# The first norm's shift and scale as TensorE products with blocks of mod_w as the stationary operand

## The chip, the cores and the metric

One NeuronCore of a Trainium2 chip runs the whole kernel. The metric is the device time of one execution in microseconds (us), the median of several runs. The engines are TensorE (PE; its weight loads stand apart as PEld), VectorE (DVE), ScalarE (ACT), GpSimd (POOL) and SyncE (SP), whose queue issues most transfers.

## What is computed

One layer of a hybrid encoder on x of 1024 tokens by 1024 columns, f32. Only its first lines matter here:

```python
mod = (jax.nn.silu(c) @ mod_w[l] + mod_b[l])[:, None, :]
sh1, sc1, g1, sh2, sc2, g2 = jnp.split(mod, 6, axis=-1)
h = rms_norm(x, norm_mix_w[l]) * (1.0 + sc1) + sh1
proj = h @ w_in[l]
...
```

c is one vector of 1024, mod_w is 1024 x 6144. What follows (gated DeltaNet heads, sparse attention, output projection, 32 experts) takes some 2600 us and needs h first. sh1 and sc1 are the first 2048 columns of mod.

## The kernel before

The host lays mod_w out as 24 blocks of [128, 8, 256]: block n holds columns 256n to 256n+255, partition p and index k together are row 128k + p. A block is 1 MB and comes in one transfer. Blocks 0 to 7 make the shift (0 to 3) and the scale (4 to 7) of the first norm, in `phase1`; blocks 8 to 23 are used later, by `later_mod`, while the projections run.

The silu of c lies in a [128, 8] tile (cs2, also self.cs), column k for rows 128k to 128k+127. The matrix-vector product of a block is made in two steps. `gemv` (line 563) multiplies each of the 8 slices [128, 256] by its column of cs2 and adds them into two accumulators (gacc): the first slice of each on ACT (line 574), the other six on DVE (line 572). Then PE sums over the partitions: for each half j of the block and each accumulator h, a product with 128 columns of the accumulator as the stationary operand and a column of ones as the moving one (line 277), so that 128 results stand down the partitions of a PSUM tile of 16 columns, `pab` (named "big" in the profile, as the pool's other tiles). That is 4 products for a block, 32 in all.

Behind the 8 blocks DVE adds the bias to `pab` (ab, line 287) and makes the scale (sca, line 289). The input x comes in 8 tiles of 128 tokens (x0 to x7). `norm` handles four of them: a square with a sum on ACT (junk, line 256), the reciprocal root in 13 short operations on DVE (`rstd`, result rs), the scaling of x on ACT (line 259). PE transposes the scaled tiles (line 317); ACT applies scale and shift to each transposed row of 512 tokens (hrow, line 319); DVE splits it into a high and a low part (hTh, hTl). With these the small projection (w_small, lines 198 to 200, as three products each) and then the index queries follow, half by half of the tokens.

The blocks use three buffers: blocks 2 and 5 one of their own (raw3), the others the pool's two (raw), which the weights w_small and w_in use next. A transfer into a buffer waits until the last reader of it is done, and SP issues its transfers in order.

Each engine works through its own list in order. The lists are not the order of the code: a scheduler of the programming layer places each instruction by its own estimate of when its operands are there.

Of the kernel before, what the change touches and what calls it, by code (L numbers as in the profile page):

```python
# [10 lines left out]
F32 = mybir.dt.float32  # L11
# [3 lines left out]
AF = mybir.ActivationFunctionType  # L15
# [5 lines left out]
P = 128  # L21
# [3 lines left out]
KD = D // P  # L25
# [109 lines left out]
class K:  # L135
# [66 lines left out]
    def phase1(self):  # L202
        nc, tc, A = self.nc, self.tc, self.A
        with ExitStack() as es:
            hp = es.enter_context(self.pool("p1h", 1))
            raw = es.enter_context(self.pool("p1raw", 2))
# [4 lines left out]
            st = esA.enter_context(self.pool("p1a", 2))  # L211
# [40 lines left out]
            def norm(half):  # L252
                s = slice(4 * half, 4 * half + 4)
                for i in range(4 * half, 4 * half + 4):
                    junk = st.tile([P, D], F32, name="junk", bufs=1)
                    nc.scalar.activation(junk, xs[i], AF.Square, accum_out=ss[:, i:i + 1])
                self.rstd(rs[:, s], ss[:, s], 1.0 / D, st)
                for i in range(4 * half, 4 * half + 4):
                    nc.scalar.activation(xs[i], xs[i], AF.Copy, scale=rs[:, i:i + 1])
# [9 lines left out]
            pab = pbig.tile([P, T], F32, name="big")  # L269

            for n in range(8):
                for i in ([0], [1], [2], [3], [], [], [], [])[n]:
                    nc.sync.dma_start(xs[i], A['x'][i * P:(i + 1) * P, :])
                acc = self.gemv(raw, st, n, 2)
                for j in range(2):
                    for h in range(2):
                        nc.tensor.matmul(pab[:, 2 * n + j:2 * n + j + 1], acc[:, h, j * P:(j + 1) * P], self.ones,
                                         start=(h == 0), stop=(h == 1))
                if n == 3:
                    norm(0)  # L280
            w_small = load_w(A['w_small'], 96)
# [29 lines left out]
            for half in range(2):  # L311

                c = slice(512 * half, 512 * half + 512)
                for k in range(KD):
# [3 lines left out]
                    h = st.tile([P, 512], F32, name="hrow", bufs=3)  # L318
# [12 lines left out]
            st = esB.enter_context(self.pool("p1b", 2))  # L331
            sc = {b: scp.tile([P, P * (b + 1)], F32, name=f"score{b}") for b in range(2, NT)}
            pl = pmm.tile([P, 512], F32, name="mm")
            for i in range(NT):
                nc.tensor.matmul(pl[:, i * 32:(i + 1) * 32], sm[64:96, i * P:(i + 1) * P], self.ident[64:96, 64:96],
                                 start=True, stop=True)
# [47 lines left out]
            st = es.enter_context(self.pool("p1c", 2))  # L384
# [3 lines left out]
            mods = []  # L388

            def later_mod():  # L390
                n = self.modn
                if n < 24:
                    self.modn += 1
                    mods.append((n, self.gemv(raw, st, n, 1)))
                if mods and (len(mods) > 1 or n == 24):
                    n, acc = mods.pop(0)
                    row = st.tile([1, 256], F32, name="mrow", bufs=2)
                    nc.sync.dma_start(row, A['mod_b'][:, n * 256:(n + 1) * 256])
                    ps = pmm.tile([P, 512], F32, name="mm")
                    nc.tensor.matmul(ps[0:1, :256], self.ones, acc[:, 0], start=True, stop=True)  # L400
                    nc.vector.tensor_tensor(row, row, ps[0:1, :256], op=ALU.add)
                    nc.gpsimd.dma_start(self.dM[n // 4 - 2:n // 4 - 1, (n % 4) * 256:(n % 4) * 256 + 256], row)
# [99 lines left out]
            def early():  # L502
                for g in order[:8]:
                    if self.group > 1:
                        later_mod()
                    yield from group(g)

            def late(groups):
                for g in groups:
                    later_mod()  # L510
                    yield from group(g)
                    later_mod()
                    if self.group == 9:
                        sums()
                        rows = tp.tile([P, T + 3], F32, name="xpad")[0:24, 0:T]
                        nc.scalar.copy(rows, ssq[0:24])
                        nc.sync.dma_start(self.dS, rows)

                        sr = tp.tile([P, T + 3], F32, name="xpad")
                        ss, rr = sr[0:96, 0:256], sr[0:96, 256:512]  # L520
                        four = lambda t: t.rearrange("r (a c) -> (r a) c", c=256)
                        nc.sync.dma_start(ss, four(self.dS))
                        self.rstd(rr, ss, 1.0, st)
                        nc.vector.tensor_scalar(rr[0:16], rr[0:16], 128 ** -0.5, None, op0=ALU.mult)
                        nc.sync.dma_start(four(self.dRQ), rr)
                    if self.group == 10:
                        self.gdn_setup(self.mp, tp, pmm)
# [3 lines left out]
            a, b = self.topk(sc, tp)  # L531
# [28 lines left out]
            nc.vector.scalar_tensor_tensor(a, a, -0.5, v, op0=ALU.mult, op1=ALU.mult)  # L560
            nc.vector.scalar_tensor_tensor(r if it == 2 else yf, a, 1.5, yf, op0=ALU.add, op1=ALU.mult)

    def gemv(self, raw, st, n, h):

        nc = self.nc
        r = st.tile([P, KD, 256], F32, name="raw3", bufs=1) if n in (2, 5) else raw.tile([P, KD, 256], F32, name="raw")
        nc.sync.dma_start(r, self.A['mod_w'][n])
        acc = st.tile([P, h, 256], F32, name="gacc", bufs=2)
        for k in range(KD):
            a = acc[:, k % h]  # L570
            if k >= h:
                nc.vector.scalar_tensor_tensor(a, r[:, k], self.cs[:, k:k + 1], a, op0=ALU.mult, op1=ALU.add)
            elif h == 2:
                nc.scalar.activation(a, r[:, k], AF.Copy, scale=self.cs[:, k:k + 1])
            else:
                nc.vector.tensor_scalar(a, r[:, k], self.cs[:, k:k + 1], None, op0=ALU.mult)
        return acc
# [1172 lines left out]
```

## Time and profile before

| | us |
|---|---|
| median of 3 runs (lowest, highest) | 2677.97 (2675.49, 2684.34) |
| the profiled execution | 2678.66 |
| its span, first to last instruction | 2677.0 |
| PE busy | 2415.7 (90%) |
| DVE busy | 1944.5 (73%) |
| ACT busy | 1522.0 (57%) |

A row of a timeline gives start and duration in us, the engine, the line, the operation, what it writes and reads, and how many instructions are merged in it; in brackets the idle time of the engine before it and what ended that. A row by stretches gives start and end, their distance, the busy time (and count) of PE, PEld, DVE, ACT and POOL, TensorE's granted clock as a share of full speed, the busy share of the 16 DMA engines, and the GB/s that they moved. A row of a group gives busy time, the mean of one in ns, and the idle time before them with its releasers. For PE, a matmul instruction on f32 operands can stand as several records.

### The profile page before, as it was taken

What the parts mean: (1) busy time and instruction counts of PE and PEld (TensorE: products, weight loads), DVE (VectorE), ACT (ScalarE), POOL (GpSimd) and SP (SyncE); (2) the same over time, 40 slices, a digit from 0 to 9 for tenths busy, and PEclk for the clock granted to TensorE, in tenths of its full rate; (3) what the DMA queues carried; (4) which work ended last, traced back from release to release, by engine and by line L of the source; (5) the groups of instructions that cost most, each with busy time, mean ns of one, the idle gap of its engine ahead of it and who ended that gap; (6) DMA issues with size and microseconds to landing.
All of it is one profiled execution on the core that took longest, in us unless ns stands there. A gap on an engine that the chain in (4) does not pass through costs nothing.

```text
span 2677.0 us, 36018 instructions
## 1 busy us (share of the span) xinstructions
PE 2415.7 (90%) x11702; PEld 1896.7 (71%) x11702; DVE 1944.5 (73%) x3547; ACT 1522.0 (57%) x2450; POOL 530.9 (20%) x423
## 2 busy tenths in 40 slices
PE   6999989788987978999999998999999999899996
PEld 4877778777876866677677766666666776677774
DVE  6687886378885887886877676588888766775653
ACT  6558323267665226775666555567667556564542
POOL 0033321244432332011110111111011101110110
PEclk9999999989999988999999999999999999999998
DMA  8123345544414338996877675599899856785731
GB/s 317 48 85 129 111 164 189 170 126 119 134 47 160 125 150 319 330 338 255 293 269 268 217 282 200 184 332 329 326 335 325 303 199 252 262 292 194 269 135 25
DMA packets 144840, 575.97 MB, mean 215 GB/s; under 512 B 35540, under 2 KB 61172, under 8 KB 89252
## 3 DMA queue, kind: packets, MB, share of 16 engines
q1 hardware_dynamic: 111876, 496.33, 51.0%
q0 software_dynamic: 19792, 48.61, 7.4%
q10 hardware_dynamic: 12880, 27.30, 2.8%
q8 instruction: 164, 2.69, 0.4%
q14 instruction: 128, 1.05, 0.1%
HBM read 534.89 MB, written 54.57 MB: 220 GB/s over the span
## 4 chain that ended last, share of the span: by engine, by line
issue 50%; PE 12%; DMA 11%; DVE 7%; POOL 4%; ACT 1%; another core or an unknown queue 1%; POOLq 0%; SPq 0%; ACTq 0%; DVEq 0%
DMA out_dram<-y,L 5%; POOL xg L1596 3%; DMA dL<-pair,rdest 2%; DMA xg<-dH,L 2%; PE tr L1143 2%; DVE Xb L929 1%; PE mm L198 1%; PE big L198 1%; PE big L199 1%; PE big L200 1%; PE mm L199 1%; PE mm L200 1%; PE lg L1116 1%; DVE tb L927 1%
## 5 line engine op out<-in xcount | busy, mean ns | idle before, releaser
L1668 PE MATMUL m<-hi,xT 128*128 128x512 f32 x2464 | 834.1, 400 | 32.5 <-DVE xT L1611 6.0
L192 DVE TENSOR_TENSOR lo<-raw,hi 128x1024 fp32r<-128x1024 f32 x471 | 556.3, 1219 | 107.4 <-ACT hi L191 86.5
L1668 PEld LDWEIGHTS m<-hi,xT 128*128 128x128 f32 x2464 | 460.0, 189 | 175.6 <-issue 51.2
L1668 PE MATMUL m<-lo,xT 128*128 128x512 f32 x1344 | 534.1, 399 | 15.3 <-issue 4.9
L191 ACT CAST hi<-raw 128x1024 fp32r<-128x1024 f32 x471 | 476.9, 1047 | 124.0 <-PEq L1522 89.6
L1668 PE MATMUL m<-hi,aT 128*128 128x512 f32 x1232 | 430.1, 409 | 19.2 <-ACT hi L191 10.4
L192 DVE TENSOR_TENSOR lo<-yT,hi 128x1024 fp32r<-128x1024 f32 x304 | 359.7, 1219 | 60.6 <-ACT hi L191 47.4
L191 ACT CAST hi<-yT 128x1024 fp32r<-128x1024 f32 x304 | 307.1, 1046 | 76.1 <-PEq L1522 58.3
L1668 PEld LDWEIGHTS m<-lo,xT 128*128 128x128 f32 x1344 | 254.1, 189 | 91.1 <-issue 27.4
L1596 POOL DMA_INDIRECT xg<-dH,L x63 | 95.3, 1512 | 1079.8 <-PE tr L1608 988.5
L1668 PEld LDWEIGHTS m<-hi,aT 128*128 128x128 f32 x1232 | 231.1, 190 | 81.1 <-ACT hi L191 16.6
L1668 PE MATMUL m<-lo,aT 128*128 128x512 f32 x672 | 274.0, 409 | 14.7 <-DVE lo L192 9.9
L1600 POOL DMA_INDIRECT out_dram<-y,L x41 | 114.2, 2787 | 342.9 <-DVE y L1729 250.9
L1709 ACT ACTIVATE act<-m,c 128x256 f32<-128x256 f32 x140 | 66.2, 473 | 191.8 <-PE m L1668 191.7
L1668 PEld LDWEIGHTS m<-lo,aT 128*128 128x128 f32 x672 | 128.3, 191 | 62.5 <-DVE lo L192 24.7
L198 PE MATMUL mm<-hTh,wh 128*128 128x512 f32 (+2 forms) x400 | 155.8, 390 | 1.8 <-ACT xpad L467 1.1
L199 PE MATMUL mm<-hTl,wh 128*128 128x512 f32 (+2 forms) x400 | 154.1, 385 | 0.0
L200 PE MATMUL mm<-hTh,wl 128*128 128x512 f32 (+2 forms) x400 | 153.8, 385 | 0.0
L1700 DVE TENSOR_TENSOR uh<-m,uh 64x512 f32<-64x512 f32 x42 | 28.7, 683 | 129.2 <-ACT uh L1699 126.1
L1094 POOL TENSOR_TENSOR L<-Tb,mask 128x128 f32<-128x128 f32 (+3 forms) x64 | 84.6, 1322 | 163.1 <-PE tr L1133 105.3
L1711 DVE TENSOR_SCALAR m<-m 128x256 f32<-128x256 f32 x140 | 59.7, 426 | 78.1 <-ACT act L1709 78.1
L1699 ACT COPY uh<-m 64x512 f32<-64x512 f32 x42 | 24.5, 584 | 135.5 <-PE m L1668 123.9
(469 smaller groups left out, 4169.5 us busy)
## 6 DMA issues: line engine op xcount, KB each, us to landing
raw<-in_w_dram SPq DMA_DIRECT2D x232, 1024.0 KB
yT<-in_w_dram SPq DMA_DIRECT2D x148, 1024.0 KB
raw<-in_mod_w_dram SPq DMA_DIRECT2D x24, 1024.0 KB
raw<-in_w_in_dram SPq DMA_DIRECT2D x16, 1024.0 KB
dU<-stage ACTq DMA_DIRECT2D x12, 512.0 KB
dT<-dF SPq DMA_DIRECT2D x8, 576.0 KB
x<-in_x_dram SPq DMA_DIRECT2D x8, 512.0 KB
dQK<-stage ACTq DMA_DIRECT2D x8, 512.0 KB
```

Of the source, the lines that this page charges most:

```text
L191: nc.scalar.copy(hi, raw)
L192: nc.vector.tensor_tensor(lo, raw, hi, op=ALU.subtract)
L198: nc.tensor.matmul(ps, xh(k), yh(k), start=(k == 0), stop=False)
L199: nc.tensor.matmul(ps, xh(k), yl(k), start=False, stop=False)
L200: nc.tensor.matmul(ps, xl(k), yh(k), start=False, stop=(k == n - 1))
L1094: nc.gpsimd.tensor_tensor(L[:, :n], Tb[:, t0:t0 + n], self.masks[b], op=ALU.add)
L1143: nc.tensor.matmul(po[:, 0:64], PT[t // 4][:, t % 4], pv[:, t, pe], start=(t == 0), stop=(t == pb))
L1596: self.nc.gpsimd.indirect_dma_start(out=xg, out_offset=None, in_=self.dH[:, :], in_offset=bass.IndirectOffsetOnAxis(ap=ix, axis=0), bounds ...
L1600: self.nc.gpsimd.indirect_dma_start(out=self.out[:, :], out_offset=bass.IndirectOffsetOnAxis(ap=ix[:z], axis=0), in_=y[:z], in_offset=None ...
L1668: mm = lambda l, r, start, stop: nc.tensor.matmul(ps, l, r, start=start, stop=stop, skip_group_check=True)
L1709: nc.scalar.activation(r, ug, AF.Relu, bias=k.c7[:z, 0:1], scale=-1.0)
L1711: nc.vector.tensor_scalar(ul, ul, 7.0, -7.0, op0=ALU.min, op1=ALU.max)
```

## The change

For blocks 0 to 7 the step through ACT and DVE is left out. PE takes each [128, 128] piece of the block as it lies in the buffer as the stationary operand and the matching column of cs2 as the moving one, and sums over k in PSUM: 2 x 8 products for a block. `gemv` stays for blocks 8 to 23, with one accumulator as before.

```diff
             for n in range(8):
...
-                acc = self.gemv(raw, st, n, 2)
+                r = st.tile([P, KD, 256], F32, name="raw3", bufs=1) if n in (2, 5) else raw.tile([P, KD, 256], F32, name="raw")
+                nc.sync.dma_start(r, A['mod_w'][n])
                 for j in range(2):
-                    for h in range(2):
-                        nc.tensor.matmul(pab[:, 2 * n + j:2 * n + j + 1], acc[:, h, j * P:(j + 1) * P], self.ones,
-                                         start=(h == 0), stop=(h == 1))
+                    for k in range(KD):
+                        nc.tensor.matmul(pab[:, 2 * n + j:2 * n + j + 1], r[:, k, j * P:(j + 1) * P], cs2[:, k:k + 1],
+                                         start=(k == 0), stop=(k == KD - 1))
...
-    def gemv(self, raw, st, n, h):
+    def gemv(self, raw, st, n):
...
-        acc = st.tile([P, h, 256], F32, name="gacc", bufs=2)
+        acc = st.tile([P, 1, 256], F32, name="gacc", bufs=2)
...
-            elif h == 2:
-                nc.scalar.activation(a, r[:, k], AF.Copy, scale=self.cs[:, k:k + 1])
```

The scheduler's lists change with it, in the part ahead of the queries. The list of PE up to the last product for `pab`, before (cs_155 is cs2, x_119 to x_122 are x0 to x3):

```order
L238 MATMUL mm<-buck,rb 8x384
L277 MATMUL big<-ones,gacc 128x1 x12
L317 MATMUL mm<-ident,x_119 128x128 x2
L277 MATMUL big<-ones,gacc 128x1
L317 MATMUL mm<-ident,x_119 128x128 x2
L277 MATMUL big<-ones,gacc 128x1 x3
L317 MATMUL mm<-ident,x_120 128x128 x4
L317 MATMUL mm<-ident,x_121 128x128 x4
L317 MATMUL mm<-ident,x_122 128x128 x4
L277 MATMUL big<-ones,gacc 128x1 x16
```

and with the change (the product is line 278, the transposes line 318):

```order
L278 MATMUL big<-cs_155,raw 128x1 x16
L238 LDWEIGHTS rb
...
L238 MATMUL mm<-buck,rb 8x384
L278 MATMUL big<-cs_155,raw 128x1 x16
L278 MATMUL big<-cs_155,raw_201 128x1 x16
L278 MATMUL big<-cs_155,raw 128x1 x16
L318 MATMUL mm<-ident,x_119 128x128 x4
L318 MATMUL mm<-ident,x_120 128x128 x4
L278 MATMUL big<-cs_155,raw 128x1 x16
L318 MATMUL mm<-ident,x_121 128x128 x4
L318 MATMUL mm<-ident,x_122 128x128 x4
L278 MATMUL big<-cs_155,raw_283 128x1 x16
L278 MATMUL big<-cs_155,raw 128x1 x32
```

The first block's products now stand ahead of the three bias products of line 238, and 16 transposes stand between the blocks' products as before. The list of ACT around the first rows of h, before (x_123 to x_126 are x4 to x7):

```order
L256 ACTIVATE junk,ss<-x_123 128x1024
L574 ACTIVATE gacc<-raw,cs_155 128x256 x2
L256 ACTIVATE junk,ss<-x_124 128x1024
L319 ACTIVATE hrow<-mm,ab,sca 128x512
L191 CAST wh<-raw 128x8x96
L319 ACTIVATE hrow<-mm,ab,sca 128x512
L256 ACTIVATE junk,ss<-x_125 128x1024
L319 ACTIVATE hrow<-mm,ab,sca 128x512
L256 ACTIVATE junk,ss<-x_126 128x1024
```

and with the change:

```order
L259 ACTIVATE x_122<-x_122,rs 128x1024
L320 ACTIVATE hrow<-mm,ab,sca 128x512 x3
L191 CAST wh<-raw 128x8x96
L320 ACTIVATE hrow<-mm,ab,sca 128x512
L256 ACTIVATE junk,ss<-x_123 128x1024
L320 ACTIVATE hrow<-mm,ab,sca 128x512
L256 ACTIVATE junk,ss<-x_124 128x1024
L320 ACTIVATE hrow<-mm,ab,sca 128x512
L256 ACTIVATE junk,ss<-x_125 128x1024
L320 ACTIVATE hrow<-mm,ab,sca 128x512
L256 ACTIVATE junk,ss<-x_126 128x1024
```

The squares of x4 and x5 stood ahead of the first row of h; now all four stand behind the fourth. SP's list has the transfers of x4 and x5 between the last two blocks and w_small before, and those of x4 to x7 behind w_small now.

## Rows read from the trace of the kernel before

**Rows 1.** The page's 40 slices of the span, PE's busy share in tenths.
```profile
PE   6999989788987978999999998999999999899996
```
**Rows 2.** Busy time by stretches of 10 us.
```profile
10.00:20.00 10.00, 3.73 (x16) 3.56 (x16) 6.25 (x16) 6.82 (x14) 0.59 (x2) 1.00 1.02 414
...
30.00:40.00 10.00, 7.28 (x33) 6.75 (x31) 7.84 (x20) 4.00 (x8) 0.00 (x0) 1.00 0.89 304
...
80.00:90.00 10.00, 10.00 (x64) 9.04 (x63) 4.57 (x15) 4.59 (x8) 0.00 (x0) 1.00 0.00 0
```
**Rows 3.** Waits from 0 to 41 us: total, times, longest.
```profile
DVE gacc L572 <- ACT gacc L574: 14.0, 5, 7.6
...
PE big L277 <- DVE gacc L572: 10.3, 6, 3.4
...
ACT gacc L574 <- DMA raw<-in_mod_w_dram: 5.1, 3, 1.9
```
**Rows 4.** Timeline of the first 41 us: first block, two bursts, ab, h.
```profile
10.21 0.91 ACT L574 ACTIVATE gacc<-raw,cs 128x256 f32<-128x256 f32 x2 [1.92 <-DMA raw<-in_mod_w_dram]
...
12.87 1.78 PEld L277 LDWEIGHTS big<-ones,gacc 128*128 128x128 f32 x8 [4.08 <-DVE gacc L572]
...
38.59 1.87 PE L277 MATMUL big<-ones,gacc 128*128 128x1 f32 x8 [1.70 <-DVE gacc L572]
...
40.50 0.17 DVE L287 TENSOR_TENSOR ab<-big,mbT 128x16 f32<-128x16 f32 x1 [1.56 <-PE big L277]
...
40.91 0.78 ACT L319 ACTIVATE hrow<-mm,ab,sca 128x512 f32<-128x512 f32 x1 [2.63 <-DVE sca L289]
```
**Rows 5.** Groups of instructions from 0 to 41 us.
```profile
L572 DVE SCALAR_TENSOR_TENSOR gacc<-raw,cs,gacc 128x256 f32<-128x256 f32 x48 | 19.6, 480 | 14.0 <-ACT gacc L574 14.0
...
L277 PEld LDWEIGHTS big<-ones,gacc 128*128 128x128 f32 x64 | 14.4, 326 | 12.3 <-DVE gacc L572 12.3
L574 ACT ACTIVATE gacc<-raw,cs 128x256 f32<-128x256 f32 x16 | 7.1, 498 | 9.4 <-DMA raw<-in_mod_w_dram 5.1 <-PE big L277 2.9 <-DVE rsa L559 1.3
...
L317 PE MATMUL mm<-ident,x 128*128 128x128 f32 x16 | 4.2, 429 | 2.0 <-ACT x L259 2.0
```
**Rows 6.** Stretches again: PE busy in the first stage, and the router's product.
```profile
24.60:32.20 7.60, 7.37 (x32) 6.52 (x32) 5.25 (x15) 4.73 (x8) 0.00 (x0) 1.00 0.75 276
...
870.00:872.00 2.00, 1.55 (x8) 1.58 (x8) 1.20 (x1) 0.77 (x1) 1.21 (x2) 0.50 0.59 156
```
**Rows 7.** Timeline of PE: bias products, transposes, two 512-column products, the router's product.
```profile
8.38 1.12 PE L238 MATMUL mm<-buck,rb 96*8 96x384 bf16 x3 [8.38 <-POOL rb L234]
...
27.51 2.80 PE L317 MATMUL mm<-ident,x 128*128 128x128 f32 x12
...
48.32 0.63 PE L200 MATMUL mm<-hTh,wl 128*96 128x512 f32 x1
...
49.78 0.39 PE L198 MATMUL mm<-hTh,wh 128*96 128x512 f32 x1
...
870.45 2.74 PE L1274 MATMUL mm<-rw,cT 128*128 128x32 f32 x12 [6.96 <-DMA cT<-dM]
```
**Rows 8.** The router's product by its line: duration of one in ns, least/median/most.
```profile
L1274 PE MATMUL mm<-rw,cT x16: 255/401/402, 870.5 to 874.5; 128*128 128x32 f32 x16
```
**Rows 9.** Timeline: a square of the second half, its scaling, the first query.
```profile
32.99 1.04 ACT L256 ACTIVATE junk<-x 128x1024 f32<-128x1024 f32 x1
33.94 0.19 ACT L256 ACTIVATION_READ_ACCUMULATOR junk<-x 128x1 f32 x1
...
52.29 0.15 DVE L561 SCALAR_TENSOR_TENSOR rs<-rsa,rsy 128x4 f32<-128x4 f32 x1
...
52.48 4.27 ACT L259 ACTIVATE x<-x,rs 128x1024 f32<-128x1024 f32 x4 [1.50 <-DVE rs L561]
...
69.79 0.38 PE L198 MATMUL mm<-hTh,wh 128*128 128x256 f32 x1
```
**Rows 10.** Weight loads of later transposes, group of the whole span.
```profile
L1719 PEld LDWEIGHTS tr<-ident,act 128*128 128x128 f32 x280 | 38.9, 139 | 18.3
```

More of the change, by code (lines that the diff above doesn't have):

```diff
@@ L393, in later_mod @@
                     self.modn += 1
-                    mods.append((n, self.gemv(raw, st, n, 1)))
+                    mods.append((n, self.gemv(raw, st, n)))
                 if mods and (len(mods) > 1 or n == 24):
@@ L561, in rstd @@
             nc.vector.scalar_tensor_tensor(r if it == 2 else yf, a, 1.5, yf, op0=ALU.add, op1=ALU.mult)
-    def gemv(self, raw, st, n, h):
+    def gemv(self, raw, st, n):
         nc = self.nc
-        r = st.tile([P, KD, 256], F32, name="raw3", bufs=1) if n in (2, 5) else raw.tile([P, KD, 256], F32, name="raw")
+        r = raw.tile([P, KD, 256], F32, name="raw")
         nc.sync.dma_start(r, self.A['mod_w'][n])
-        acc = st.tile([P, h, 256], F32, name="gacc", bufs=2)
+        acc = st.tile([P, 1, 256], F32, name="gacc", bufs=2)
         for k in range(KD):
-            a = acc[:, k % h]
-            if k >= h:
+            a = acc[:, 0]
+            if k:
                 nc.vector.scalar_tensor_tensor(a, r[:, k], self.cs[:, k:k + 1], a, op0=ALU.mult, op1=ALU.add)
-            elif h == 2:
-                nc.scalar.activation(a, r[:, k], AF.Copy, scale=self.cs[:, k:k + 1])
             else:
```

## The prediction

> **What bounds the kernel now.** I start with the page's slices of 67 us: TensorE (PE) is busy nine or ten tenths in nearly all of them, and six tenths in the first [rows 1]. So the change is at the one place where PE is not the bound, and a delay there moves everything behind it. The table by stretches of 10 us shows the same more closely: PE has 3.73 of 10 us between 10 and 20, 7.28 between 30 and 40, and from 80 on it is full; the transfers take all of the sixteen DMA engines in the first of these stretches (a share of 1.02) and 0.89 in the second [rows 2]. The list of waits says who holds whom in the first 41 us: PE's products wait 10.3 us for the sums on VectorE (DVE), these 14.0 us for the first two products on ScalarE (ACT), and those 5.1 us for the blocks of mod_w [rows 3]. DMA feeds ACT, ACT feeds DVE, DVE feeds PE, and PE has time to spare. The timeline gives the ends of this stage: the first block is there at 10.21 (ACT starts), PE's last column of shift and scale ends at 38.59 + 1.87 = 40.46, the vector ab is made at 40.50 from it, and at 40.91 the first row of the normalized input follows [rows 4]. **The stage lasts 30.25 us from the first block to PE's last column**, and that is what the change replaces.
>
> **What is removed.** 48 sums on DVE of 0.480 us (23.0 us when added up) and 16 scalings on ACT of 0.498 us (8.0 us), and on PE the 32 short products, which the profile shows as 64 passes, two for each product [rows 5]. None of the 31 us on DVE and ACT comes back as such: it lay beside the transfers, and both engines waited in the stage [rows 3].
>
> **What is added.** Each of the 8 blocks now needs 2 x 8 products with a 128x128 f32 block as the stationary operand and one moving column: 128 products, and at two passes each 256 passes instead of 64. The form is the one that the profile shows already (128x128 stationary, 128x1 moving, f32), so its price is in the rows. A pass is a weight load with a column behind it, and the loads follow each other without a gap inside a burst: 8 of them take 1.78 us [rows 4], one 0.326 on the mean [rows 5], so the step is (1.78 - 0.326) / 7 = 0.208 us. The router's product further on has the same loads with 32 moving columns: 12 passes in 2.74 us [rows 7]; one alone 0.401 [rows 8], so 2.34 / 11 = 0.213 us. All loads of this form in the stage, each burst's head included, give 14.4 / 64 = 0.225 us [rows 5]. Lower bound 0.208, upper 0.225; I take 0.213, the longest burst, since the new bursts are of 32. 256 x 0.213 = **54.5 us of PE alone, in a stage that has 30.25**.
>
> [...]
>
> Is PE's list in the way too? By the new order the first block's products come ahead of the three bias products (1.12 us), and 16 transposes of x lie between the blocks: 12 of them take 2.80 us [rows 7], one 0.43 [rows 5], so the step is (2.80 - 0.43) / 11 = 0.215, and 16 make 3.4 us. They were in the stage before, in PE's gaps; now there are no gaps. Blocks arrive faster than they are used: one block is 1.05 MB, 2.5 us at the 414 GB/s of [rows 2], against 32 x 0.213 = 6.8 us on PE, and three buffers hold them. So from 10.2 on PE has no gap: 10.2 + 54.5 + 1.1 + 3.4 + 0.2 (the last column's way out) = **69.4 instead of 40.46: 28.9 us later**. What was late before (DVE's sums) is gone; what is late next is PE itself.
>
> **Behind the stage.** Up to the second half of x, ACT's list decides. Before, the squares of x4 and x5 came ahead of the first row of h (the first at 32.99), in time that ACT had; the second half's scaling started at 52.48, 0.04 us after rs, which is 12.0 us behind ab [rows 9]. In the new order all four squares stand behind the first rows of h, although ACT will idle for much of the stage. So ACT has two squares more between ab and rs, each 1.04 us and 0.19 for reading its sum [rows 9]: **2.5 us more**, with the rest as before. Bounds: 0, if ACT and DVE find the room in their waits, and 4.0, if they lose once more the 1.50 that ACT waited for rs [rows 9]. The x tiles themselves now are issued behind w_small, which waits for the seventh block's buffer, 7 us ahead of PE's last column; 2.5 MB take 6 us at 414 GB/s, so x4 is there when ACT comes to it, and SP holds nothing else back. The cast of w_in's first block waits for the eighth block's buffer now as before. From the queries (69.78 [rows 9]) on the lists of all engines are the same, and PE is full there [rows 2], so nothing takes the delay up.
>
> **Sum.** 28.9 + 2.5 = 31.4 us. The profiled execution took 2678.66 us (span 2677.0 and 1.66 around it), 0.7 over the median of the three runs shown; 2678.66 + 31.4 = 2710.1, or 2709.4 from the median. I say 2710.
>
> **Rivals.**
>
> *PE's clock rises during the products.* [...] The nearest price at full clock is that of the transposes, 0.139 us for one with its load [rows 10]; half of 0.213 is 0.107. [...] Against it: from 24.6 to 32.2 PE was busy 7.37 of 7.60 us with transposes and just these products [rows 6], and the burst at 38.59 still took 1.87 us, no less than the eight loads at 12.87 with 1.78 [rows 4]. I give it 0.08, half of it within 0.3%.
>
> [...]
>
> *The transfers are the bound, and the change is not slower.* If a block's 32 passes hid behind the next block's transfer, PE would end one block behind the last landing. From 10.21 there remain 7 blocks and 3 x tiles, 8.9 MB, at 414 GB/s 21.5 us; with 2.5 us for the last block 34.2 instead of 40.46, and with ACT's 2.5 the end is 3.8 us earlier, 2675. This is decided at a pass of 2.5 / 32 = 0.079 us. For it speaks that ACT waited for blocks before [rows 3], and that two engines are taken out of the line; against it that no f32 load in the rows has a step under 0.139, even at full clock [rows 10]. 0.02.
>
> *Something faster that I don't see* (the freed DVE and ACT, or a different mix behind the stage): 0.02.
>
> **How the numbers follow.** My case has 0.88. Its range: 256 passes at 0.208 to 0.225 (53.2 to 57.6), ACT's term 0 to 4: 2678.66 + 28.9 - 1.3 = 2706 to 2678.66 + 28.9 + 3.1 + 4 = 2715, and some us on either side for where the clock rises later and for the runs' own spread (2675.5 to 2684.3): **2700 to 2718**. The rivals lie below it with 0.12. A measurement of this kernel tells about 0.3%, 8 us, from no change. Slower by more: 0.88 + 0.04. Within: 0.04 + 0.02. Faster: 0.02.
>
> **What would show it.** Right: 256 passes of the new product, in bursts of 32 that last about 6.8 us; PE without a gap from 10.2 to about 69; ab near 69.5; DVE nearly empty and ACT idle up to there; the second half's scaling 14 to 15 us behind ab; from the queries on the same distances as before, 31 us later. Wrong: weight loads that fall to half the time in mid-stage (the clock), gaps of PE that end on a block of mod_w (the transfers), or a last column well ahead of 66.

## The result and the profile after

The changed kernel took 2704.64 us, the median of six runs (2702.28 to 2718.84), against 2678.01 for the kernel before in six runs on the same chip (2675.49 to 2684.34). The ratio is 1.0112 (95% interval 1.0084 to 1.014): slower by 0.8 to 1.4%. I had predicted 2710 with a range of 2700 to 2718.

The profiled execution of after is a long one: 2717.98 us, its span 2716.3. So its first stage can be read from it, but not its total. The page's slices answer to [rows 1]: the first slice went from six tenths to eight, and otherwise the page looks as before.

```profile
PE   8999988988888897999999989999999999999996
```

The timeline from 0 to 72 us answers to [rows 4] and, in its last row, to [rows 9]:

```profile
11.00 6.96 PE L278 MATMUL big<-cs,raw 128*128 128x1 f32 x32 [11.00 <-DMA raw<-in_mod_w_dram]
17.89 1.12 PE L238 MATMUL mm<-buck,rb 96*8 96x384 bf16 x3
18.94 20.56 PEld L278 LDWEIGHTS big<-cs,raw 128*128 128x128 f32 x96 [0.64 <-issue]
...
39.44 1.95 PE L318 MATMUL mm<-ident,x 128*128 128x128 f32 x8
...
41.18 6.83 PE L278 MATMUL big<-cs,raw 128*128 128x1 f32 x32
...
47.87 1.95 PE L318 MATMUL mm<-ident,x 128*128 128x128 f32 x8
...
49.61 20.48 PE L278 MATMUL big<-cs,raw 128*128 128x1 f32 x96
70.12 0.17 DVE L288 TENSOR_TENSOR ab<-big,mbT 128x16 f32<-128x16 f32 x1 [44.72 <-PE big L278]
...
83.45 4.27 ACT L259 ACTIVATE x<-x,rs 128x1024 f32<-128x1024 f32 x4 [0.73 <-DVE rs L562]
...
101.32 0.38 PE L198 MATMUL mm<-hTh,wh 128*128 128x256 f32 x1
```

Read it downwards. From 11.0 on PE's bursts follow each other with no idle time in brackets: products, the bias products, transposes, products. A burst of 96 passes takes 20.56, so a pass takes (20.56 - 0.333) / 95 = 0.213 us (0.333 is the mean load, in the group below). DVE has waited 44.7 us for PE when it makes ab at 70.12, and the first query is at 101.32 instead of 69.79.

The group of the new product has the 256 passes, 55 us, and as its only wait the first block. In [rows 5], the old products had 64 passes and waited 12.3 us for DVE:

```profile
L278 PEld LDWEIGHTS big<-cs,raw 128*128 128x128 f32 x256 | 55.0, 333 | 11.6 <-issue 11.6
L278 PE MATMUL big<-cs,raw 128*128 128x1 f32 x256 | 54.9, 351 | 11.0 <-DMA raw<-in_mod_w_dram 11.0
```

The list of waits up to 75 us shows the line of [rows 3] turned round: DVE and ACT wait for PE, and no block is waited for but the first.

```profile
DVE ab L288 <- PE big L278: 44.7, 1, 44.7
ACT hrow L320 <- DVE sca L290: 40.9, 1, 40.9
...
PE big L278 <- DMA raw<-in_mod_w_dram: 11.0, 1, 11.0
```

The table by stretches of 10 us (columns as in [rows 2]: PE, PEld, DVE, ACT, POOL, granted clock, DMA share, GB/s) says the same in busy time. Between 30 and 40 PE has 10.00 of 10 us where it had 7.28, DVE and ACT have nothing, and the DMA engines are at 0.30 instead of 0.89. Between 80 and 90, where PE was full, it now waits in between, for the second half of x and of h.

```profile
10.00:20.00 10.00, 9.00 (x40) 8.18 (x41) 0.00 (x0) 1.59 (x4) 0.19 (x2) 1.00 0.88 332
...
30.00:40.00 10.00, 10.00 (x48) 10.00 (x49) 0.00 (x0) 0.00 (x0) 0.00 (x0) 1.00 0.30 107
...
80.00:90.00 10.00, 5.97 (x22) 2.86 (x21) 6.50 (x18) 9.23 (x12) 0.00 (x0) 0.75 1.04 316
```

### The profile page after: what moved, and what is told of

It reads as the page before. It is cut to its first block, busy times and chain, and to the rows that moved or that the text cites. A ratio compares the mean times of both kernels' runs of the same rounds, so it can differ in the third digit from the quotient of the medians.

```text
span 2716.3 us, 36315 instructions
## 1 busy us (share of the span) xinstructions
PE 2467.7 (91%) x11894; PEld 1948.4 (72%) x11894; DVE 1925.6 (71%) x3499; ACT 1513.7 (56%) x2434; POOL 531.0 (20%) x423
## 4 chain that ended last, share of the span: by engine, by line
issue 50%; PE 12%; DMA 11%; DVE 6%; POOL 4%; another core or an unknown queue 1%; ACT 1%; POOLq 0%; SPq 0%; ACTq 0%; DVEq 0%
DMA out_dram<-y,L 5%; POOL xg L1595 3%; DMA dL<-pair,rdest 2%; DMA xg<-dH,L 2%; PE tr L1142 1%; PE big L200 1%; PE big L198 1%; PE big L199 1%; PE mm L198 1%; PE mm L200 1%; PE mm L199 1%; DVE Xb L928 1%; PE lg L1115 1%; DVE tb L926 1%
## 5 line engine op out<-in xcount | busy, mean ns | idle before, releaser
L1667 PE MATMUL m<-hi,aT 128*128 128x512 f32 x1232 | 436.3, 415 | 19.3 <-ACT hi L191 10.4
L1667 PE MATMUL m<-lo,aT 128*128 128x512 f32 x672 | 279.5, 417 | 15.6 <-DVE lo L192 11.0
L1722 ACT CAST aT<-tr 128x256 fp32r<-128x256 f32 (+1 forms) x168 | 58.3, 347 | 82.9 <-PE tr L1718 82.4
```

What stands on the lines that cost most here:

```text
L1667: mm = lambda l, r, start, stop: nc.tensor.matmul(ps, l, r, start=start, stop=stop, skip_group_check=True)
L1722: nc.scalar.copy(hi, p2)
```

## The experiments

Two things were to be told apart. The first was the price of a pass: is it that of f32 weight loads at a granted clock of 0.50, as the router's product has them with the same step of 0.213 us, and can a clock of 1.00 be had? The second was what takes part of the delay back: the first query is 31.5 us late in the profile, the medians differ by 26.6.

Before was measured anew beside each group of runs: its median was 2678.01 beside after, 2682.29 beside the four runs from half of the products to early squares, 2680.47 beside block as moving operand, upper half words, one block of eight and after again, and 2678.75 beside the two runs with two bf16 words. The third column compares with that one. The times in the last column come from one profile of each kernel.

| run | us, median (range, runs) | over before | first block's products, ab, first query at |
|---|---|---|---|
| before, profile | 2678.01 (2675.49 to 2684.34, 6) | | 10.2 (ACT), 40.5, 69.8 |
| after, profile | 2704.64 (2702.28 to 2718.84, 6) | 26.6 | 11.0, 70.1, 101.3 |
| half of the products | 2776.49 (1) | | 9.7, 42.0, 72.9 |
| dense products ahead | 2707.09 (2703.7 to 2714.09, 4) | 24.8 | 11.3, 67.7, 98.8 |
| dense products between | 2724.57 (2721.84 to 2724.67, 4) | 42.3 | 9.6, 84.3, 114.9 |
| early squares | 2704.7 (2702.4 to 2713.71, 4) | 22.4 | 9.9, 66.0, 91.8 |
| block as moving operand | 2684.51 (2680.47 to 2693.5, 10) | 4.0 | 9.7, 48.1, 76.4 |
| upper half words | 2673.57 (1) | | 10.5, 34.0, 64.5 |
| one block of eight on PE | 2679.0 (2673.14 to 2681.59, 12) | -1.5 | -, 45.7, 69.7 |
| two bf16 words | 2675.44 (2672.12 to 2682.82, 11) | -3.3 | 9.5, 36.2, 68.1 |
| two bf16 words, early x | 2673.29 (2669.56 to 2676.92, 11) | -5.5 | 9.9, 41.0, 69.1 |
| after again | 2704.6 (2704.06 to 2718.17, 7) | 24.1 | 10.6, 69.7, 100.2 |

**Half of the products.**

```diff
-                    for k in range(KD):
+                    for k in range(4):
...
-                                         start=(k == 0), stop=(k == KD - 1))
+                                         start=(k == 0), stop=(k == 3))
```

> The changed kernel with only the first four of the eight k of each block's products, so half of the shift's and scale's sum is left out (the experts' load then depends on other numbers, so only the first 110 us are read). Theory: the stage is PE's passes and nothing else, 0.213 us each; 128 passes less are 27.3 us less, the vector ab at 70.1 - 27.3 = 42.8 us and the first query near 74. Rival: the transfers of the blocks, their buffers or the transposes between them hold the stage as well; then ab comes at 50 or later.

The timeline has ab 32.3 us behind the first product, where after has 59.15:

```profile
9.68 3.55 PE L278 MATMUL big<-cs,raw 128*128 128x1 f32 x16 [9.68 <-DMA raw<-in_mod_w_dram]
...
42.00 0.17 DVE L288 TENSOR_TENSOR ab<-big,mbT 128x16 f32<-128x16 f32 x1 [19.56 <-PE big L278]
```

128 passes less are worth 59.15 - 32.32 = 26.8 us, 0.210 each: the stage is the number of passes times their price. The total (2776.49) can't be used: with half of the sum missing h has other values, and the stage of the experts, to which tokens are sent by these values, is some 98 us longer.

**Dense products ahead.** 32 products of 512 bf16 columns run on PE while it waits for the first block, so that the new products begin with the clock up.

```diff
+            wt = st.tile([P, 512], BF, name="wt", bufs=1)
+            nc.vector.memset(wt, 0.5)
+            dense = pbig.tile([P, T], F32, name="big")
...
+            def warm(m):
+                for i in range(m):
+                    nc.tensor.matmul(dense[:, 0:512], wt[:, 0:P], wt, start=True, stop=True)
+            warm(32)
```

> The changed kernel with 32 products of 512 bf16 columns on PE ahead of the first block, while PE waits for it, so that its clock is up when the stage begins. [...]

The first 32 passes took 4.21 us instead of 6.96, the 96 behind them 20.64 as before, and ab came at 67.71. I had expected 66 to 70 with the step of 0.21 back early in the stage, and 42 to 51 if a step of 0.11 to 0.14 lasted through it. By stretches (columns as above):

```profile
12.00:13.00 1.00, 1.00 (x11) 1.00 (x10) 0.00 (x0) 0.00 (x0) 0.00 (x0) 1.00 1.00 422
13.00:14.00 1.00, 1.00 (x11) 1.00 (x10) 0.00 (x0) 0.00 (x0) 0.00 (x0) 1.00 0.99 406
14.00:15.00 1.00, 1.00 (x8) 1.00 (x7) 0.00 (x0) 0.00 (x0) 0.00 (x0) 0.60 1.10 459
...
16.00:18.00 2.00, 2.00 (x9) 1.47 (x8) 0.00 (x0) 2.00 (x4) 0.51 (x1) 0.50 0.97 391
```

Ten loads per us at a granted clock of 1.00 are 0.1 us a pass. Then the clock falls, to 0.60 between 14 and 15 **while PE and its loads are busy without a gap**, and to 0.50 between 16 and 18. So the price is 0.1 at a granted clock of 1.00 and 0.213 at 0.50 (as at the router), and the clock fell during these products. By this I don't take the 1.00 that the column of [rows 2] has in the stage of before and after for a measured level: the step there is the router's at 0.50.

**Dense products between.** Behind every second product stands one bf16 product of 512 columns, with a tile of zeros as the stationary operand.

```diff
...
+                        if k % 2 == 1:
+                            nc.tensor.matmul(dense[:, 0:512], wt, r.bitcast(BF)[:, k - 1:k + 1, 1::2], start=True, stop=True)
```

> The changed kernel with one product of 512 bf16 columns (read from the same block) behind every second product of the stage, 64 in all, whose results nobody reads. [...] Rival: the clock stays down in this stage whatever PE does; then the additions cost 64 times 0.43 us and ab comes near 98, the total 27 us above the changed kernel.

Neither number came: ab is behind the 57 to 66 that I had expected with passes of 0.107 to 0.139 us, and ahead of the rival's 98. The timeline shows the pattern:

```profile
10.45 0.59 PE L284 MATMUL big<-raw,wt 128*128 128x512 bf16 x1
10.83 0.85 PE L281 MATMUL big<-cs,raw 128*128 128x1 f32 x4
11.54 0.59 PE L284 MATMUL big<-raw,wt 128*128 128x512 bf16 x1
```

From one dense product to the next it is 1.09 us, four passes (0.852) and 0.24; ab came at 84.27, 74.7 us behind the first product. By the step the clock stayed down: four passes still take 0.85 us, 0.213 each. The additions cost 74.7 - 59.15 = 15.5 us, 0.24 each, and not the 0.43 of the rival: in the trace the next pass starts 0.38 us behind the start of the dense product (10.45, 10.83), ahead of the end of its record. Only stationary zeros were tried here.

**Early squares.** x4 to x7 are loaded between the blocks and squared there, to take ACT's work out from behind ab.

```diff
...
-                for i in ([0], [1], [2], [3], [], [], [], [])[n]:
+                for i in ([0], [1], [2], [3], [4], [5], [6], [7])[n]:
...
+                if n > 3:
+                    junk = st.tile([P, D], F32, name="junk", bufs=1)
+                    nc.scalar.activation(junk, xs[n], AF.Square, accum_out=ss[:, n:n + 1])
...
-            for i in range(4, NT):
-                nc.sync.dma_start(xs[i], A['x'][i * P:(i + 1) * P, :])
```

> The changed kernel with x4 to x7 loaded ahead of blocks 4 to 7 and their squares written into the loop over blocks, so that ACT and DVE do the whole norm while PE makes the products. Theory: behind ab ACT's list decides, and four squares (5.0 us) and four scalings (4.3 us) leave it; ab stays at 70.1, the way from ab to the first query falls from 31.2 to 22 to 26 us, and the total is 5 to 9 us under the changed kernel. Rival: DVE's splits or PE's transposes decide there; then the way stays near 31 us and the total is the same.

From ab to the first query it is 25.75 us instead of 31.2, and ab itself comes at 66.03. The scheduler's list now has all 16 transposes in one go (38.35 to 42.00), and behind them the clock was up: 20 passes in the first 2 us, 11 in the third 2 us, in the middle of one burst of 128:

```profile
42.00:44.00 2.00, 2.00 (x20) 2.00 (x19) 0.00 (x0) 0.00 (x0) 0.00 (x0) 1.00 0.90 358
44.00:46.00 2.00, 2.00 (x18) 2.00 (x18) 0.11 (x1) 1.15 (x2) 0.00 (x0) 0.89 0.01 2
46.00:48.00 2.00, 2.00 (x11) 2.00 (x11) 1.66 (x11) 0.00 (x0) 0.00 (x0) 0.50 0.56 143
```

The first query is 7.7 to 9.5 us earlier than in the four profiles of after. In the medians less of it is seen: 22.4 us over the before beside it, where after has 26.6 and 24.1, so 1.7 to 4.2 us, and that with four executions; 5 to 9 were expected. This is the second question, taken up below.

**Block as moving operand.** The column of cs2 is stationary and the block's 256 columns move; the row of results is turned into two columns by two one-column products.

```diff
+                if n % 4 == 0:
+                    rows = pbig.tile([P, T], F32, name="big")
+                o = slice(256 * (n % 4), 256 * (n % 4) + 256)
+                for k in range(KD):
+                    nc.tensor.matmul(rows[0:1, o], cs2[:, k:k + 1], r[:, k], start=(k == 0), stop=(k == KD - 1))
+                row = st.tile([1, 256], F32, name="abrow", bufs=2)
+                nc.vector.tensor_copy(row, rows[0:1, o])
                 for j in range(2):
-                    for k in range(KD):
...
+                    nc.tensor.matmul(pab[:, 2 * n + j:2 * n + j + 1], row[0:1, j * P:(j + 1) * P], self.ones[0:1, 0:1],
+                                     start=True, stop=True)
```

> The changed kernel with the operands' roles exchanged: the column of cs2 is stationary (a load of one column), the block's 256 columns move; the row that comes out is copied by DVE and turned into two columns by two small products. 64 products of two passes. [...]

Half as many passes, each with 256 columns:

```profile
24.99 3.61 PE L280 MATMUL big<-raw,cs 128*1 128x256 f32 x16
28.54 0.77 PE L324 MATMUL mm<-ident,x 128*128 128x128 f32 x5
```

A pass takes 0.22 us here, as much as a one-column pass of after, so 22 us of the 29.6 came back (ab at 48.15, where 46 to 52 were expected). The transposes between them were faster too: 5 took 0.77, where 8 of after took 1.95. By that I take the clock to be up; the column has 1.00 from 20 to 48 us, 0.72 from 48 to 53 and 0.50 from 53 to 57. The ratio to before is 1.001 (0.9994 to 1.0026), and 20 to 23 us of after's delay are gone, where 16 to 24 were expected.

**Upper half words.** The block's upper bf16 halves alone are the stationary operand, and the column is rounded to bf16.

```diff
+            cb = st.tile([P, KD], BF, name="cb", bufs=1)
+            nc.vector.tensor_copy(cb, cs2)
...
+                rb16 = r.bitcast(BF)
...
-                        nc.tensor.matmul(pab[:, 2 * n + j:2 * n + j + 1], r[:, k, j * P:(j + 1) * P], cs2[:, k:k + 1],
+                        nc.tensor.matmul(pab[:, 2 * n + j:2 * n + j + 1], rb16[:, k, 2 * j * P + 1:2 * (j + 1) * P:2], cb[:, k:k + 1],
```

> The changed kernel with bf16 operands: of each number of the block only the upper 16 bits, and cs2 rounded, so shift and scale lose accuracy; read by its first 110 us. Theory: the price of a product is two f32 weight loads of 0.213 us; a bf16 product has one pass, and its load takes half, so 128 passes of about 0.107 us are 14 us, less than the transfers of the blocks, and ab comes at 36 to 42 us. Rival: a load of 128 columns takes 0.21 us whatever its type; then 128 passes are 27 us and ab comes at 42 to 46.

```profile
10.54 0.58 PE L281 MATMUL big<-cb,raw 128*128 128x1 bf16 x16 [10.54 <-DMA raw<-in_mod_w_dram]
...
14.38 0.58 PE L281 MATMUL big<-cb,raw 128*128 128x1 bf16 x16 [2.21 <-DMA raw<-in_mod_w_dram]
...
33.39 0.58 PE L281 MATMUL big<-cb,raw 128*128 128x1 bf16 x16 [3.48 <-DMA raw<-in_mod_w_dram]
```

Sixteen bf16 products with their loads take 0.58 us, 0.036 each, where the same sixteen in f32 take 32 passes and 6.9 us. The theory's price (0.107) was three times too high, the rival's (0.21) six times. PE now waits 22.9 us for blocks (10.5 of them for the first), the last one too, and ab comes at 34.01: the transfers are the bound, which the prediction's second rival had put at 34.2.

**One block of eight on PE.** The kernel before, with only block 4 by the new product and x4 to x7 early.

```diff
...
+                if n in (4,):
...
+                            nc.tensor.matmul(pab[:, 2 * n + j:2 * n + j + 1], r[:, k, j * P:(j + 1) * P], cs2[:, k:k + 1],
+                                             start=(k == 0), stop=(k == KD - 1))
+                else:
+                    acc = self.gemv(raw, st, n, 2)
...
```

> The kernel before with two things of the experiments: block 4 alone goes through PE's direct products (32 passes, 6.8 us, in the stretch where ACT scales the first half of x), and x4 to x7 are loaded early with their squares and scalings inside the stage. Theory: ab at 39 to 44 us and 26 us from there to the first query instead of 29.3, so the first query at 65 to 69 instead of 69.8 us, and the total 1 to 5 us under the kernel before, less than its own spread. Rival: with eight squares and scalings beside the blocks ACT becomes the bound of the stage; ab at 46 or later, and the total 2 us or more above the kernel before.

ab at 45.69 and the first query at 69.70 against 69.79; ratio 0.9985 (0.9973 to 0.9997). At the first query nothing was gained: ab came behind the theory's 39 to 44 us, just ahead of the rival's 46.

**Two bf16 words.** DVE subtracts the upper half of each f32 from the whole and leaves the rest as bf16. Both parts are stationary operands; the column of cs2 moves as two bf16 columns, and two sums make ab.

```diff
...
+                hi = r.bitcast(BF)[:, :, 1::2]
                 for j in range(2):
+                    lo = st.tile([P, KD, P], BF, name="wlo", bufs=2)
+                    m = slice(j * P, (j + 1) * P)
+                    nc.vector.tensor_tensor(lo, r[:, :, m], hi[:, :, m], op=ALU.subtract)
+                    for x in range(2):
+                        for k in range(KD):
+                            nc.tensor.matmul(pab[:, 4 * n + 2 * j:4 * n + 2 * j + 2], lo[:, k] if x else hi[:, k, m], cb[:, k],
+                                             start=(x == 0 and k == 0), stop=(x == 1 and k == KD - 1))
...
```

> The changed kernel with each number of a block as two bf16 numbers: its upper 16 bits as they lie in the buffer, and the rest, which DVE subtracts (two operations of [128, 8, 128] for a block) and rounds to bf16; cs2 likewise as two columns, so that a product has two moving columns and DVE adds two results of 16 columns. 32 bf16 passes for a block instead of 32 f32 passes. Theory: the f32 form of the load is the whole price; with bf16 passes (16 in 0.58 us in the run with upper halves alone) PE needs about 1.1 us for a block, DVE 2.4, the transfers 2.5 to 3.9, so that the stage is bound by transfers and DVE, ab at 36 to 39 us, 30 us from there to the first query, and the total 1 to 5 us under the kernel before. Rival: DVE reads the upper halves with a stride and takes over 2 us for each of its two operations; then DVE is the bound, ab at 45 or later, and the total is over the kernel before.

```profile
L285 DVE TENSOR_TENSOR wlo<-raw 128x1024 bf16<-128x1024 f32 x16 | 19.2, 1239 | 10.6 <-DMA raw<-in_mod_w_dram 9.5 <-PE big L288 0.9
...
L288 PE MATMUL big<-cb,wlo 128*128 128x2 bf16 x128 | 6.1, 168 | 7.4 <-DVE wlo L285 7.4
L288 PE MATMUL big<-cb,raw 128*128 128x2 bf16 x128 | 5.8, 166 | 12.3 <-DMA raw<-in_mod_w_dram 12.3
```

256 passes are 12 us of PE now. ab comes at 36.19, and the median is 2675.44, ratio to before 0.9992 (0.9978 to 1.0005). So it isn't that the sum is made on PE that made after slow, but the price of its f32 passes.

**Two bf16 words, early x** adds the early squares' edit to this (split_words in the text below is the run just shown).

> As split_words, with x4 to x7 loaded between the blocks and their squares and scalings inside the stage. Theory: four more x tiles put 5 us of transfers into the stage, ab at 39 to 43 us; 25 to 26 us from ab to the first query as when the squares were early; first query at 64 to 68 instead of 69.8, total 2 to 6 us under the kernel before. Rival: what is gained behind ab is lost ahead of it; total as split_words or above.

ab at 41.00, the first query at 69.08 where 64 to 68 were expected, and 2673.29 us: 0.998 of before (0.9971 to 0.9989), and by the ratios some 28 to 35 us less than after. It is the best of the kernels that compute the whole, by a fifth of a per cent over before. But only 0.7 of these 5.5 us are there at the first query; its profile is 2.9 us shorter than before's between the router and the experts; more on that place below.

**After again**, three times: once with more runs, twice for one more profile (the second and third repeat below).

> The changed kernel once more, unchanged. Theory: up to the router (its first weight load at 870.4 us before) the delay is the same in every execution, 31 to 32 us; what lies behind it, the router's and the experts' stages, differs between executions by some us either way whatever the change does, so that the times spread from about 2702 to 2719 around 2678 + 31 = 2709. Rival: the change itself gives some 5 us back behind the router; then every execution of this run lies at 2702 to 2706, and the long ones seen once do not come again.

> The changed kernel unchanged, for a profile of one of its shorter executions. Theory: with a time near 2704 the router's first weight load comes at 901 to 903 us as in the other two profiles, and the experts' stage (from its first tile to the end) takes 1665 to 1668 us instead of 1678.5. Rival: the short executions are short ahead of the router already.

> The changed kernel unchanged, a second look beside again_b. Theory: a short execution has its router at 901 to 903 us and an experts' stage of 1665 to 1668 us, a long one the same router and 1678 us or more. Rival: they part ahead of the router.

The seven runs have a ratio of 1.0084 (1.0065 to 1.0102); the other two took 2704.68 and 2699.6. Of all 15 executions of after 3 are at 2718, 2 at 2710 and 10 at or below 2705.3. So the long ones did come again, against the rival, but the delay at the router isn't the same in every execution either: 31.4 us in after's profile, 32.2, 28.8 and 25.5 in the repeats. With three points of the profiles (first query; first weight load of the router; first cast of the experts' tiles) the executions divide like this:

| us | first query | to the router | to the experts | to the end | span |
|---|---|---|---|---|---|
| before | 69.8 | 800.6 | 138.5 | 1668.0 | 2677.0 |
| after | 101.3 | 800.5 | 135.6 | 1678.9 | 2716.3 |
| after again | 100.2 | 802.5 | 135.4 | 1678.4 | 2716.5 |
| second repeat | 99.5 | 799.7 | 135.4 | 1668.4 | 2703.0 |
| third repeat | 100.4 | 795.6 | 135.4 | 1666.5 | 2697.9 |

Two things stand out. First, before's own profile is 3 us longer between router and experts than 12 of the other 13 profiles of this study, which have 135.2 to 135.7. The thirteenth, that of dense products between, has 138.4. The place is the last update of x on DVE, which waits there for a store to land, in before and in dense products between:

```profile
978.79 1.29 DVE L1291 TENSOR_TENSOR x<-big,g1b 128x512 f32<-128x512 f32 x2 [3.82 <-DMA out_dram<-x]
1024.08 1.29 DVE L1295 TENSOR_TENSOR x<-big,g1b 128x512 f32<-128x512 f32 x2 [3.81 <-DMA out_dram<-x]
```

and for a product of PE in after, 29.2 us behind before instead of the 31.4 at the router:

```profile
1007.95 1.29 DVE L1290 TENSOR_TENSOR x<-big,g1b 128x512 f32<-128x512 f32 x2 [1.19 <-PE big L200]
```

Second, the two of the executions at 2718 that have a profile lose some 10 us among the experts. Between 1640 and 1800 the long one (after's profile)

```profile
1640.00:1720.00 80.00, 73.33 (x288) 54.67 (x287) 45.17 (x65) 38.33 (x60) 9.00 (x4) 0.89 0.50 178
1720.00:1800.00 80.00, 73.60 (x289) 54.01 (x287) 50.12 (x67) 42.00 (x63) 7.60 (x5) 0.91 0.66 222
```

has a lower granted clock and fewer products than the second repeat in the same stretch of its work:

```profile
1637.00:1717.00 80.00, 73.53 (x303) 55.14 (x302) 46.59 (x65) 38.71 (x62) 7.79 (x3) 0.94 0.53 186
1717.00:1797.00 80.00, 73.19 (x309) 53.61 (x307) 55.79 (x75) 47.36 (x70) 8.48 (x5) 1.00 0.72 248
```

PE is busy for the same time and does 288 and 289 products instead of 303 and 309. The execution of after again that has a profile took 2718.17 us, with 1678.4 in the same part; its granted clock over the whole is 0.965, that of after's profile 0.964, that of the second repeat 0.970. Why the clock is lower there in some executions stays open; the same source has both.

## Why the prediction was right, and where it was off

**What bounds the kernel** was right: PE waited in the first stage, and the delay from there stands whole at the router in after's profile (901.81 - 870.45 = 31.4 us).

**The price of a pass** was right: 0.213 us predicted, 0.213 measured, and 0.210 per pass taken away. At a granted clock of 1.00 the run with dense products ahead showed about 0.1.

**The stage.** 59.2 us were predicted from the first block to the end of the sums, and 59.15 measured up to ab. ab came at 70.12, and of these 29.6 us 0.76 are a first block that landed later in this execution (10.97 against 10.21); in the table of the runs the first products start between 9.5 and 11.3.

**ACT's two squares** were over-sized: 2.5 us predicted, within bounds of 0 and 4. The scaling starts 13.33 us behind ab instead of 11.98, 1.35 more (14 to 15 were forecast), and the first query follows 31.20 us behind ab instead of 29.29, 1.91 more; in the three repeats it is 1.2 more. ACT found some of the room in its waits (0.73 us for rs, 1.50 before). At the first query the sum was 31.4, measured 31.5. That they agree so closely is partly luck: the late first block and the smaller term of ACT cancel, and the repeats have 29.7 to 30.6.

**The clock rival** (0.08) fell. 59 us of unbroken work left the step at 0.213, and a clock that was up fell from 1.00 to 0.50 in the middle of PE's work (dense products ahead between 13 and 18 us, early squares between 42 and 48). So in this stage, with one moving column, unbroken work neither brought the clock up nor held it. For a clock that rises later, which the range counts with some us, no run shows a figure: where the step of the 512-column products falls from 0.43 to 0.23 us in before (starts at 48.75 and 49.18, at 50.02 and 50.25), the column has 1.00 throughout, and in after the step is 0.23 from the second of these products on (76.18 and 76.41). **The transfer rival** (0.02) was far from deciding, as its own condition said (0.079 us per pass against 0.213). Its 34.2 came near the 34.01 measured with cheap passes, but by luck: the last block was there at 33.39 instead of the 31.7 worked out, and its products took 0.6 us instead of 2.5.

**The step that was off** is "nothing takes the delay up" behind the queries, together with a sum made against one execution. The delay is 29.7 to 31.5 at the first query in the four profiles of after and 25.5 to 32.2 at the router, but the medians differ by 26.6 and, in the longer comparison, by 24.1. The second repeat took 2704.68, which is about after's median, and its row shows where the rest went against before's profile: 29.7 later at the first query, then 0.9 shorter up to the router, 3.1 shorter up to the experts and 0.4 longer behind, 26.0 in all. The 3.1 are at the update of x that waited for a store in before; I took that execution as typical because its total was 0.7 over the median. Whether before waits there in most executions isn't shown, since it has one profile. For it speaks that in eight of the nine rows of the runs' table that give a difference the median lies 1.4 to 6.3 us less over before than the first query; early squares are the ninth, with 22.4 against 22.0. All nine use the one first query of before, though, and a shift of that would look the same. The other stages differ for one and the same kernel: from the first query to the router after took 795.6 to 802.5 us, among the experts 1666.5 to 1678.9. What sets these lengths wasn't found. All this moved the result by 5 us, inside the range.

## What to carry to other kernels

Where the matrix is the stationary operand, price a matrix-vector product on TensorE by its passes, not by its columns: in f32 each 128x128 piece cost two passes of 0.213 us here, the step that the router's product has with 32 moving columns, and it stayed at 0.213 through the 59 us of the stage. If such a product must go to TensorE, let the matrix move (22 of 29.6 us came back) or give it as bf16 words (256 passes in 12 us instead of 55). And look first whether the engines that it frees were the bound: DVE and ACT gave up 31 us of work in the stage, and the stage became twice as long.

## What the runs showed of the hardware that I had not expected

- An f32 product with its weight loads cost far more than twice a bf16 one: sixteen with one column took 6.9 us in f32 (32 passes) and 0.58 in bf16 (16 passes), twelve times less, and six times less for a pass. At which clock the bf16 loads ran isn't shown; at a granted clock of 1.00 an f32 pass took 0.1 us, still nearly three times 0.036.
- TensorE's granted clock went down from 1.00 during unbroken one-column products, twice, with no idle time of PE or its loads: to 0.60 between 14 and 15 us with dense products ahead, to 0.50 between 46 and 48 with early squares. With one 512-column product behind every four passes the step stayed at 0.21; behind sixteen transposes in a row there were 20 passes in 2 us, and with the block as the moving operand 5 transposes took 0.77 us.
- A product of 512 columns between such passes cost 0.24 us and not the 0.59 of its record; in the trace the next pass starts 0.38 us behind its start.
- DVE's subtraction of a strided bf16 view from f32 (1024 columns to bf16) took 1.24 us on the mean, so that the split of a block took some 2.5 us, and DVE still waited 9.5 us for blocks, 5.8 of them for the first.
